# Gated attention levels dealt out head by head between quarters of projection units, with two modulation columns moved one stage later

## The chip, the cores and the metric

The kernel runs on one core of one Trainium2 chip. The metric is the device time of one execution in microseconds; less is better. The core has a matrix engine (TensorE, PE in the rows, its weight loads PEld), a vector engine (VectorE, DVE), a scalar engine (ScalarE, ACT), GpSimd (POOL), and SyncE (SP), whose queue issues almost all transfers from memory.

## The reference, cut to what matters

Two decoder layers over 512 positions of width 1024, in float32. Layer 0 mixes tokens with gated linear attention, layer 1 with latent attention; each is followed by a SwiGLU block, and each sub-layer is normalised and modulated by columns computed from a conditioning vector `c`. Only layer 0's mixer is touched by the change:

```python
mod = silu(c) @ ada_w[i] + ada_b[i]                # 6 x 1024 modulation values per layer
sh1, sc1, g1, sh2, sc2, g2 = split(mod, 6)
h = rmsnorm(x, norm_mix) * (1 + sc1) + sh1
q, k, v, r, glr = split(h @ w_in)                  # 4 heads, DK 128, DV 256
log_a = log_sigmoid(glr @ w_gate + b_gate) / 16    # a decay per position, head and channel
# per head: attn[i, j] = sum_d q[i,d] k[j,d] exp(b[i,d] - b[j,d]) for j <= i, b = cumsum(log_a)
o = rmsnorm(attn @ v, g_out) * silu(r)
x = x + g1 * (o @ w_out)
h = rmsnorm(x, norm_ffn) * (1 + sc2) + sh2          # the next sub-layer needs sc2, sh2
```

## The kernel before, in words

Activations lie transposed, 128 features by 512 positions per tile. Every product is made to float32 accuracy from three passes in a faster type (`mm3`, L178 to L180): each operand is split into a high and a low part, and high x high, high x low and low x high are summed in PSUM. A weight unit (`wunit`, L156) is 128x1024 floats: one load on SP's queue, one cast on ScalarE (L164, `wh`), one subtraction on VectorE (L172, `wl`). Raw, `wh` and `wl` have three buffers each. A unit feeds 24 matmuls of 512 columns.

The gated attention avoids a recurrence by seven **levels** (`LEVELS`, block sizes 1 to 64). At each level and for each of the 4 heads, `level` (L647) multiplies small blocks of k and q on TensorE (16 matmuls of 32x16 for the first five levels, 8 and 4 larger ones for the last two) into a PSUM bank `lv`; VectorE copies the result out (L670, L644), and `decay` (L672) scales half of the rows of q and k on VectorE (L680, L681), which the same head's next level reads. Before the levels `head_setup` (L616) makes each head's diagonal blocks (L626) and `qf`, the decayed copy of q (L632).

The matmuls of this stretch stand in an order written by hand (`manual_schedule` for PE); VectorE, ScalarE and SP have no hand-written order here and are ordered by a scheduler. The hand-written order puts a **fill** after each level: one projection unit of 24 matmuls, so that VectorE can finish all four heads while TensorE works. The fills are the last unit of v's first half, two units of r (`r_tile`, L762), and the four units of v's second half (`v_units`, L723, a generator that yields after each unit).

After the levels come the larger off-diagonal scores (`scores_a`, `scores_b`, L692 to L706), their splits into high and low (`att_split`, `ah` and `al`), the products with v (`pv_head`, tile `pv`), six more units of r with the heads' norms between them (`o_stats`, tile `no_st`, 16 matmuls of one column), and then the output projection (`boundary`, L315): five full units, each followed by a residual update (L290), a square on ScalarE and a sum on VectorE (L268), then the last three units in two halves of 256 positions, with the norm of the first half (`nm_st`) between.

Modulation columns are made on VectorE: `ada` (L136) loads a 128x1024 tile (`adaw`, two buffers), takes its dot product with the conditioning vector (L132) and adds the bias (L141). They wait in one list (`pend_ada`), and `more_ada(n)` takes the next n from it: two in each `r_tile` from the third on, two after each of the first four residuals of the output projection (`also`, L858), three per unit in the SwiGLU block. Columns 9 to 24 of that list are the scale and shift that the SwiGLU block's `modulated` needs.

```python
fill = [lambda: next(v0), lambda: r_tile(0), lambda: r_tile(1), lambda: next(v1), ...]
for li, s in enumerate(LEVELS):
    for hd in range(H):
        level(hd, li, s)
        decay(hd, s)
    fill[li]()
```

Of the kernel before, what the change touches and what calls it, by code (L numbers as in the profile page):

```python
# [21 lines left out]
KD = D // P  # L22
NT = S // P
# [60 lines left out]
def trunk(ctx: ExitStack, tc: tile.TileContext, t: dict, out: bass.AP):  # L84
# [11 lines left out]
    def R(name, dt=F32, cols=S):  # L96
        return ring.tile([P, cols], dt, tag="ring", name=name, bufs=NRING)
# [58 lines left out]
    def wunit(src, n=1024, home=None, split_=True):  # L156
        raw = wp.tile([P, 1024], F32, tag="raw", name="raw")
        nc.sync.dma_start(out=raw[:, :n], in_=src)
        if home is None:
            wh = wp.tile([P, 1024], F32R, tag="wh", name="wh")  # L160
            wl = wp.tile([P, 1024], F32R, tag="wl", name="wl")
        else:
            wh, wl = home
        nc.scalar.copy(out=wh[:, :n], in_=raw[:, :n])  # L164
        w = (wh, wl, raw)
        if split_:
            wunit_lo(w, n)
        return w[:2] if split_ else w
# [13 lines left out]
    def sl(pair, *idx):  # L182
        return pair[0][idx], pair[1][idx]
# [432 lines left out]
    def head_setup(hd):  # L616
        d = heads[hd]
        qs, kr = qk[("q", hd)], qk[("k", hd)]
        if not dqs:
            dqs.append(R("dq"))  # L620
        dq = dqs[0][:, hd * NT * QB:(hd + 1) * NT * QB]
        ps = abank("lv0")
        for i in range(NT):
            for b in range(0, P, QB):
                c = slice(i * P + b, i * P + b + QB)
                nc.tensor.matmul(ps[b:b + QB, i * QB:(i + 1) * QB], lhsT=kr[:, c], rhs=qs[:, c],  # L626
                                 start=i == 0, stop=i == NT - 1, tile_position=(0, b))
        nc.vector.tensor_tensor(out=dq.rearrange("p (a b) -> p a b", b=QB),
                                in0=ps[:, :NT * QB].rearrange("p (a b) -> p a b", b=QB),
                                in1=kc[:, None, K_IDQ:K_IDQ + QB].to_broadcast([P, NT, QB]), op=ALU.mult)  # L630
        qf = R("qf")
        nc.vector.tensor_tensor(out=qf, in0=qs, in1=d["e1"], op=ALU.mult)  # L632
        d.update(kr=kr, qf=qf, dq=dq)
# [89 lines left out]
    def v_units(g):  # L723

        pv = [bank(f"v{i}") for i in range(NT)]
        for u in range(4):
            w = vw.pop((g, u)) if (g, u) in vw else v_load(g, u)
            for kk in range(2):
                k = 2 * u + kk
                for i in range(NT):  # L730
                    mm3(pv[i], sl(h[k], slice(None), slice(i * P, (i + 1) * P)),
                        sl(w, slice(None), slice(kk * S, (kk + 1) * S)), k == 0, k == KD - 1)
            if u == 3:
                for i in range(NT):
                    vt[(g, i)] = split(pv[i], "v")
            yield
# [23 lines left out]
    sr = {}  # L760

    def r_tile(n, cuts=()):  # L762
        w = wunit(t["gla_r"][n])
        if n > 1:
            with tc.issue_after(last["w"]):
                more_ada(2)
        ps = bank("r")
        for k in range(KD):
            mm3(ps, sl(w, slice(None), slice(k * P, (k + 1) * P)), h[k], k == 0, k == KD - 1)
            for k_, f in cuts:  # L770
                if k_ == k:
                    f()
        sr[n] = R("sr")
        nc.scalar.activation(out=sr[n], in_=ps, func=AF.Silu)

    def o_spread(hd):
        o, y = pvs[hd]
# [38 lines left out]
    more_ada(4)  # L816
    with tc.manual_schedule(engines={mybir.EngineType.PE}):
        v0, v1 = v_units(0), v_units(1)
        next(v0)
        ps = abank("qk")  # L820
        proj(ps, w3, h)
        take("k", 3, ps)
        next(v0)
        next(v0)
        for hd in range(H):
            head_setup(hd)
        fill = [lambda: next(v0), lambda: r_tile(0), lambda: r_tile(1), lambda: next(v1), lambda: next(v1),
                lambda: next(v1), lambda: next(v1)]
        for li, s in enumerate(LEVELS):
            for hd in range(H):  # L830
                level(hd, li, s)
                decay(hd, s)
            fill[li]()
        scores_a(0)
        scores_a(1)
        r_tile(2)
        scores_b(0)
        scores_b(1)
        pv_head(0)
        scores_a(2)  # L840
        r_tile(3, [(3, lambda: o_stats(0))])
        scores_b(2)
        pv_head(1)
        scores_a(3)
        r_tile(4, [(1, lambda: o_spread(0)), (3, lambda: o_stats(1))])
        o_out(0)
        scores_b(3)
        pv_head(2)
        r_tile(5, [(1, lambda: o_spread(1)), (3, lambda: o_stats(2))])
        o_out(1)  # L850
        pv_head(3)
        r_tile(6, [(1, lambda: o_spread(2)), (3, lambda: o_stats(3))])
        o_out(2)
        r_tile(7, [(1, lambda: o_spread(3))])
        o_out(3)
    oh = [oh[i] for i in range(KD)]

    def also(n):  # L858
        if n < 4:
            more_ada(2)  # L860


# [431 lines left out]
```

## Time and profile before

| | |
|---|---|
| median of 3 runs | 1183.88 us (1180.38, 1183.88, 1184.00) |
| the profiled execution | 1180.7 us, of which the span from first to last instruction is 1178.9 us |
| TensorE busy | 1154.1 us, 98% of the span, 7070 matmul records |
| VectorE busy | 724.1 us, 61% |
| ScalarE busy | 417.3 us, 35% |
| granted TensorE clock, mean | 0.996 of full speed |
| memory traffic | 130 GB/s over the span |

A small float32 matmul leaves two records, so the 16 matmuls of one head's level show as x32. A matmul's shown duration is longer than its share of the engine, since matmuls overlap; what a matmul costs is the step from its start to the next one's start. A wait is the idle time in front of an instruction, with what ended it behind an arrow; "issue" means that nothing the profile shows ended it. The stretch that the change touches is 87 to 140 us (levels), and then 140 to 248 us (scores, r units, output projection).

### The profile page before, as it was taken

The page shows a single profiled execution, that of the slowest core. Times are in us where ns is not written, and L with a number is a line of the kernel's source. Part 1 is how long each engine was busy: PE and PEld are TensorE (multiplying, and loading weights), DVE is VectorE, ACT ScalarE, POOL GpSimd, SP SyncE. Part 2 cuts the span into 40 slices and gives each one's busy share as a digit, 9 for nine tenths or more (in the row PEclk, how much of TensorE's full clock was granted, in tenths as well). Part 3 has the DMA queues.
Part 4 walks back from the last instruction along what each step waited for, and adds up shares of the span by engine and source line. Part 5 has one row for each costly group of instructions (what it writes and reads, how often), then busy time and mean ns, then how long its engine had stood idle before and what let it go on. Part 6 is the DMA issues. An engine that isn't in the chain of part 4 may idle for free.

```text
span 1178.9 us, 17489 instructions
## 1 busy us (share of the span) xinstructions
PE 1154.1 (98%) x7070; PEld 974.6 (83%) x7070; DVE 724.1 (61%) x1428; ACT 417.3 (35%) x666; POOL 18.1 (2%) x40
## 2 busy tenths in 40 slices
PE   8999999999999999999999899999999999999996
PEld 5877878898888888888899788889888888888886
DVE  6987898875763567556566878757333332333345
ACT  3372445342322222232344556534232222223231
POOL 0000000000000000000000022000000000000000
PEclk9999999999999999999999999999999999999998
DMA  9762264714663567356421224141323333233222
GB/s 355 239 194 57 79 226 127 231 55 146 226 242 101 174 236 244 117 202 231 148 86 51 78 62 107 54 126 31 95 90 97 100 91 100 95 105 93 90 71 72
DMA packets 47379, 156.91 MB, mean 133 GB/s; under 512 B 5602, under 2 KB 8034, under 8 KB 47299
## 3 DMA queue, kind: packets, MB, share of 16 engines
q1 hardware_dynamic: 45474, 153.48, 40.2%
q0 software_dynamic: 1536, 2.10, 0.8%
q8 instruction: 55, 0.90, 0.3%
q10 hardware_dynamic: 288, 0.23, 0.1%
q14 instruction: 26, 0.21, 0.0%
HBM read 151.59 MB, written 2.10 MB: 130 GB/s over the span
## 4 chain that ended last, share of the span: by engine, by line
PE 87%; DVE 7%; DMA 3%; ACT 1%; issue 1%; DVEq 0%; ACTq 0%
PE f L178 12%; PE f L180 12%; PE f L179 12%; PE op L178 9%; PE op L179 8%; PE op L180 8%; PE fg L179 2%; DMA adaw<-in_ada 2%; PE fg L178 2%; PE fg L180 2%; DVE wl L172 1%; DVE junk L132 1%; PE r L178 1%; PE v L178 1%; PE ko L179 1%; PE r L179 1%
## 5 line engine op out<-in xcount | busy, mean ns | idle before, releaser
L164 ACT CAST wh<-raw 128x1024 fp32r<-128x1024 f32 (+2 forms) x173 | 177.5, 1026 | 554.3 <-PE f L179 180.2
L172 DVE TENSOR_TENSOR wl<-raw,wh 128x1024 fp32r<-128x1024 f32 (+2 forms) x181 | 215.4, 1191 | 107.6 <-ACT wh L164 102.1
L178 PE MATMUL f<-hh,wh 128*128 128x512 f32 x640 | 249.0, 389 | 0.0
L179 PE MATMUL f<-hl,wh 128*128 128x512 f32 x640 | 249.0, 389 | 0.0
L180 PE MATMUL f<-hh,wl 128*128 128x512 f32 x640 | 249.0, 389 | 0.0
L178 PE MATMUL op<-acth,wh 128*128 128x512 f32 (+1 forms) x394 | 144.7, 367 | 0.0
L179 PE MATMUL op<-actl,wh 128*128 128x512 f32 (+1 forms) x394 | 144.3, 366 | 0.0
L180 PE MATMUL op<-acth,wl 128*128 128x512 f32 (+1 forms) x394 | 144.3, 366 | 0.0
L180 PEld LDWEIGHTS f<-hh,wl 128*128 128x128 f32 x640 | 120.1, 188 | 25.0
L179 PEld LDWEIGHTS f<-hl,wh 128*128 128x128 f32 x640 | 120.1, 188 | 24.9
L178 PEld LDWEIGHTS f<-hh,wh 128*128 128x128 f32 x640 | 120.1, 188 | 24.8
L290 DVE SCALAR_TENSOR_TENSOR x<-op,mod,x 128x512 f32<-128x512 f32 (+1 forms) x76 | 50.6, 665 | 124.2 <-PE op L180 123.9
L132 DVE SCALAR_TENSOR_TENSOR junk<-adaw,cact 128x1024 bf16<-128x1024 f32 x94 | 114.7, 1220 | 13.8 <-DMA adaw<-in_ada 13.7
L901 DVE TENSOR_TENSOR sg<-sg,f 128x512 f32<-128x512 f32 x40 | 27.5, 688 | 123.5 <-PE f L180 123.5
L178 PEld LDWEIGHTS op<-acth,wh 128*128 128x128 f32 x394 | 74.3, 189 | 12.2
L179 PEld LDWEIGHTS op<-actl,wh 128*128 128x128 f32 x394 | 74.3, 189 | 12.2
L180 PEld LDWEIGHTS op<-acth,wl 128*128 128x128 f32 x394 | 74.3, 189 | 12.1
L268 DVE TENSOR_TENSOR acc<-acc,sq 128x512 f32<-128x512 f32 (+1 forms) x45 | 25.1, 558 | 14.7 <-ACT sq L267 14.6
L280 ACT ACTIVATE hh<-u,mod 128x256 fp32r<-128x256 f32 (+1 forms) x49 | 23.5, 509 | 29.2 <-DVE u L277 29.2
L267 ACT ACTIVATE sq<-x 128x256 f32<-128x256 f32 (+1 forms) x38 | 19.2, 505 | 38.3 <-DVE x L290 38.2
L903 DVE TENSOR_TENSOR actl<-sg,acth 128x512 fp32r<-128x512 f32 (+1 forms) x48 | 30.8, 642 | 0.8 <-ACT acth L902 0.5
L902 ACT CAST acth<-sg 128x512 fp32r<-128x512 f32 (+1 forms) x48 | 28.1, 585 | 6.7 <-DVE sg L901 6.5
(324 smaller groups left out, 1890.8 us busy)
## 6 DMA issues: line engine op xcount, KB each, us to landing
adaw<-in_ada SPq DMA_DIRECT2D x96, 512.0 KB, 4.4
raw<-in_ffn_in SPq DMA_DIRECT2D x80, 512.0 KB, 3.7
raw<-in_ffn_o SPq DMA_DIRECT2D x32, 448.0 KB, 3.3
raw<-in_ffn_o SPq DMA_DIRECT2D x16, 512.0 KB, 3.6
raw<-in_gla_ko SPq DMA_DIRECT2D x8, 512.0 KB, 5.6
raw<-in_gla_v SPq DMA_DIRECT2D x8, 512.0 KB, 4.3
raw<-in_gla_r SPq DMA_DIRECT2D x8, 512.0 KB, 3.9
raw<-in_gla_wo SPq DMA_DIRECT2D x8, 512.0 KB, 3.7
```

What stands on the lines that cost most here:

```text
L132: nc.vector.scalar_tensor_tensor(out=junk, in0=w, scalar=1.0, in1=cact, op0=ALU.mult, op1=ALU.mult, accum_out=acc)
L164: nc.scalar.copy(out=wh[:, :n], in_=raw[:, :n])
L172: ins = nc.vector.tensor_tensor(out=wl[:, :n], in0=raw[:, :n], in1=wh[:, :n].bitcast(F32), op=ALU.subtract)
L178: nc.tensor.matmul(ps, lhsT=ah, rhs=bh, start=start, stop=False)
L179: nc.tensor.matmul(ps, lhsT=ah, rhs=bl, start=False, stop=False)
L180: nc.tensor.matmul(ps, lhsT=al, rhs=bh, start=False, stop=stop)
L268: nc.vector.tensor_tensor(out=self.acc[:, c], in0=self.acc[:, c], in1=sq[:, c], op=ALU.add)
L280: nc.scalar.activation(out=hi[:, c], in_=u[:, c], func=AF.Identity, bias=sh)
L290: ins = nc.vector.scalar_tensor_tensor(out=x[k][:, c], in0=ps[:, c], scalar=mod[l][2 + 3 * j][:, k:k + 1], in1=x[k][:, c], op0=ALU.mult, o ...
L901: ins = nc.vector.tensor_tensor(out=sg[:, c], in0=sg[:, c], in1=pu[:, c], op=ALU.mult)
L902: nc.scalar.copy(out=hi[:, c], in_=sg[:, c])
L903: nc.vector.tensor_tensor(out=lo[:, c], in0=sg[:, c], in1=hi[:, c].bitcast(F32), op=ALU.subtract)
```

## The change

`v_units` and `r_tile` become generators of quarters (six matmuls each). `steps(gen, n)` takes n quarters. In the level loop a quarter of the fill stands behind each head instead of a whole unit behind each level, and two quarters of v's third unit stand among the four head set-ups. `r_tile(2)` loses its two modulation columns, and the output projection takes two more, behind its fifth residual.

```diff
@@ v_units
                         sl(w, slice(None), slice(kk * S, (kk + 1) * S)), k == 0, k == KD - 1)
+                    if i % 2 and (kk, i) != (1, NT - 1):
+                        yield
             if u == 3:
@@
     def r_tile(n, cuts=()):
+        for _ in r_quarters(n, cuts):
+            pass
+
+    def r_quarters(n, cuts=()):
         w = wunit(t["gla_r"][n])
-        if n > 1:
+        if n > 2:
             with tc.issue_after(last["w"]):
                 more_ada(2)
...
+            if k % 2 and k < KD - 1:
+                yield
         sr[n] = R("sr")
         nc.scalar.activation(out=sr[n], in_=ps, func=AF.Silu)
+        yield
@@
-        next(v0)
+        def steps(gen, n):
+            for _ in zip(range(n), gen):
+                pass
+
+        steps(v0, 4)
         ps = abank("qk")
         proj(ps, w3, h)
         take("k", 3, ps)
-        next(v0)
-        next(v0)
+        steps(v0, 6)
         for hd in range(H):
+            steps(v0, 1 if hd < 2 else 0)
             head_setup(hd)
-        fill = [lambda: next(v0), lambda: r_tile(0), lambda: r_tile(1), lambda: next(v1), lambda: next(v1),
-                lambda: next(v1), lambda: next(v1)]
+        fill = [v0, r_quarters(0), r_quarters(1), v1, v1, v1, v1]
         for li, s in enumerate(LEVELS):
             for hd in range(H):
                 level(hd, li, s)
                 decay(hd, s)
-            fill[li]()
+                steps(fill[li], 1)
@@
     def also(n):
-        if n < 4:
+        if n < 5:
             more_ada(2)
```

On TensorE, at the head set-ups and the first level (`v` are the projection's 512-column matmuls, `lv` the small ones, - before and + after):

```order
 L180 MATMUL v_856<-wh,hl 128x512
-L626 MATMUL lv_957<-q,k 32x32 x16
 L626 MATMUL lv_977<-q,k 32x32 x16
 L626 MATMUL lv_997<-q,k 32x32 x16
 L626 MATMUL lv_1017<-q,k 32x32 x16
-L664 MATMUL lv<-qf,k 32x16 x64
+L664 MATMUL lv<-qf,k 32x16 x16
 L178 MATMUL v_853<-wh,hh 128x512
...
 L180 MATMUL v_854<-wh,hl 128x512
+L664 MATMUL lv<-qf,k 32x16 x16
 L178 MATMUL v_855<-wh,hh 128x512
```

One run of 128 small matmuls (four set-ups and the first level) becomes five runs, of 16 (moved up by six 512-column matmuls), 64, 16, 16 and 16. Each of the other six levels, one run before, becomes four. In all 7 runs become 29.

On VectorE, between the scores of the first two heads and the first product with v, before:

```order
L303 TENSOR_TENSOR al_1814<-od_a_1808,ah_1813 128x2x128
L132 SCALAR_TENSOR_TENSOR junk_1833,adac_1834<-adaw_1831,cact_79 128x1024
L172 TENSOR_TENSOR wl_1923<-raw_1920,wh_1922 128x1024
L141 TENSOR_TENSOR mod0_2_97<-adac_1834,cols_76 128x1
L132 SCALAR_TENSOR_TENSOR junk_1928,adac_1929<-adaw_1926,cact_79 128x1024
L172 TENSOR_TENSOR wl_2058<-raw_2055,wh_2057 128x1024
L141 TENSOR_TENSOR mod0_2_97<-adac_1929,cols_76 128x1
L132 SCALAR_TENSOR_TENSOR junk_1934,adac_1935<-adaw_1932,cact_79 128x1024
L303 TENSOR_TENSOR al_1803<-od_b_1864,ah_1802 128x2x256
L303 TENSOR_TENSOR al_1814<-od_b_1869,ah_1813 128x2x256
```

and now:

```order
L303 TENSOR_TENSOR al_1814<-od_a_1808,ah_1813 128x2x128
L132 SCALAR_TENSOR_TENSOR junk_1916,adac_1917<-adaw_1914,cact_79 128x1024
L172 TENSOR_TENSOR wl_2046<-raw_2043,wh_2045 128x1024
L141 TENSOR_TENSOR mod0_2_97<-adac_1917,cols_76 128x1
L132 SCALAR_TENSOR_TENSOR junk_1922,adac_1923<-adaw_1920,cact_79 128x1024
L172 TENSOR_TENSOR wl_2191<-raw_2188,wh_2190 128x1024
L303 TENSOR_TENSOR al_1803<-od_b_1852,ah_1802 128x2x256
L303 TENSOR_TENSOR al_1814<-od_b_1857,ah_1813 128x2x256
```

One dot product fewer stands ahead of `al`; the other that is gone stood in front of the last level's copies. The splits of the diagonal scores (`al<-dg`) now stand between the heads of the last level instead of behind them.

On VectorE, in the output projection behind the fifth unit's residual (`x4_84`; `x5_85` to `x7_87` are the halves that follow), before:

```order
L290 SCALAR_TENSOR_TENSOR x4_84<-op_2745,mod0_2_97,x4_84 128x512
L172 TENSOR_TENSOR wl_2789<-raw_2786,wh_2788 128x1024
L268 TENSOR_TENSOR acc_2516<-acc_2516,sq_2771 128x512
L290 SCALAR_TENSOR_TENSOR x5_85<-op_2811,mod0_2_97,x5_85 128x256
L268 TENSOR_TENSOR acc_2516<-acc_2516,sq_2837 128x256
L290 SCALAR_TENSOR_TENSOR x6_86<-op_2840,mod0_2_97,x6_86 128x256
L268 TENSOR_TENSOR acc_2516<-acc_2516,sq_2866 128x256
L290 SCALAR_TENSOR_TENSOR x7_87<-op_2869,mod0_2_97,x7_87 128x256
```

and now:

```order
L290 SCALAR_TENSOR_TENSOR x4_84<-op_2732,mod0_2_97,x4_84 128x512
L132 SCALAR_TENSOR_TENSOR junk_2763,adac_2764<-adaw_2761,cact_79 128x1024
L268 TENSOR_TENSOR acc_2503<-acc_2503,sq_2758 128x512
L141 TENSOR_TENSOR mod0_4_99<-adac_2764,cols_76 128x1
L172 TENSOR_TENSOR wl_2789<-raw_2786,wh_2788 128x1024
L149 SCALAR_TENSOR_TENSOR gs0_1_108<-mod0_4_99,cols_76 128x1
L132 SCALAR_TENSOR_TENSOR junk_2770,adac_2771<-adaw_2768,cact_79 128x1024
L290 SCALAR_TENSOR_TENSOR x5_85<-op_2811,mod0_2_97,x5_85 128x256
L141 TENSOR_TENSOR mod0_3_98<-adac_2771,cols_76 128x1
L290 SCALAR_TENSOR_TENSOR x6_86<-op_2840,mod0_2_97,x6_86 128x256
L268 TENSOR_TENSOR acc_2503<-acc_2503,sq_2837 128x256
```

Two dot products stand ahead of the first half's residual, one of them ahead of the last weight unit's `wl`. On SP's queue the second one's load stands behind the SwiGLU block's first `in_ffn_in` load.

## Rows read from the trace of the kernel before

**Rows 1.** The page's first part: busy time, share of the span, instructions.
```profile
PE 1154.1 (98%) x7070; PEld 974.6 (83%) x7070; DVE 724.1 (61%) x1428; ACT 417.3 (35%) x666; POOL 18.1 (2%) x40
```

**Rows 2.** Busy time by stretch: us, each engine, granted clock, DMA share, GB/s.
```profile
87.30:140.20 52.90, 50.98 (x1033) 41.85 (x1033) 41.35 (x112) 19.42 (x35) 0.00 (x0) 1.00 0.26 77
```

**Rows 3.** TensorE's waits, 87 to 215 us: us in total, times, longest.
```profile
PE pv L179 <- DVE al L303: 1.6, 1, 1.6
PE lv L664 <- issue: 1.0, 1, 1.0
PE lv L664 <- DVE qf L632: 0.9, 3, 0.4
PE no_st L230 <- DVE acc L268: 0.6, 2, 0.4
```

**Rows 4.** TensorE's timeline, a projection unit, then a level: start, duration, instruction.
```profile
70.98 0.39 PE L178 MATMUL qk<-hh,wh 128*128 128x512 f32 x1
...
76.19 0.39 PE L180 MATMUL qk<-hh,wl 128*128 128x512 f32 x1
...
97.83 0.39 PE L180 MATMUL v<-wh,hl 128*128 128x512 f32 x1
98.15 1.34 PE L664 MATMUL lv<-qf,k 128*32 128x16 f32 x128
99.42 0.50 PE L178 MATMUL r<-hh,wh 128*128 128x512 f32 x1
99.75 0.39 PE L179 MATMUL r<-hl,wh 128*128 128x512 f32 x1
...
105.08 1.34 PE L664 MATMUL lv<-qf,k 128*32 128x16 f32 x128
```

**Rows 5.** TensorE's timeline around the head set-ups and the first level.
```profile
87.07 0.39 PE L180 MATMUL v<-wh,hl 128*128 128x512 f32 x1
...
93.52 0.39 PE L179 MATMUL v<-wl,hh 128*128 128x512 f32 x1
```

**Rows 6.** TensorE's timeline, 16 small matmuls inside a unit of r.
```profile
192.90 0.40 PE L180 MATMUL r<-hh,wl 128*128 128x512 f32 x1
193.23 0.43 PE L230 MATMUL no_st<-ones,acc 128*32 128x1 f32 x32
...
194.64 0.40 PE L179 MATMUL r<-hl,wh 128*128 128x512 f32 x1
```

**Rows 7.** VectorE's timeline ahead of the first product with v.
```profile
148.96 1.23 DVE L132 SCALAR_TENSOR_TENSOR junk<-adaw,cact 128x1024 bf16<-128x1024 f32 x1
...
150.12 1.28 DVE L303 TENSOR_TENSOR al<-od_b,ah 128x512 fp32r<-128x512 f32 x2
```

**Rows 8.** VectorE's timeline in the output projection.
```profile
232.69 1.23 DVE L132 SCALAR_TENSOR_TENSOR junk<-adaw,cact 128x1024 bf16<-128x1024 f32 x1 [0.89 <-DMA adaw<-in_ada]
...
234.51 0.75 DVE L290 SCALAR_TENSOR_TENSOR x<-op,mod,x 128x512 f32<-128x512 f32 x1
235.17 1.22 DVE L172 TENSOR_TENSOR wl<-raw,wh 128x1024 fp32r<-128x1024 f32 x1
...
240.48 0.43 DVE L268 TENSOR_TENSOR acc<-acc,sq 128x256 f32<-128x256 f32 x1 [0.48 <-ACT sq L267]
```

**Rows 9.** TensorE's timeline in the output projection: the last unit's first half, the norm.
```profile
236.44 0.38 PE L180 MATMUL op<-ohh,wl 128*128 128x256 f32 x1 [0.18 <-DVE wl L172]
...
242.14 0.31 PE L230 MATMUL nm_st<-ones,acc 128*32 128x1 f32 x16
```

**Rows 10.** The tile adaw, 205 to 245 us: its loads.
```profile
DMA to landing us min/median/max: 3.6/4.6/5.9
```

**Rows 11.** Busy time by stretch near the end, columns as in rows 2.
```profile
1170.00:1172.00 2.00, 1.22 (x4) 0.93 (x4) 0.97 (x6) 0.00 (x0) 0.00 (x0) 0.50 0.08 26
```

**Rows 12.** TensorE's timeline near the end: the same two matmuls (four records) twice.
```profile
1163.77 0.60 PE L246 MATMUL nf_bc<-kc,rs_f 128*128 128x128 f32 x4
...
1170.67 1.22 PE L246 MATMUL nf_bc<-kc,rs_f 128*128 128x128 f32 x4 [2.45 <-DVE rs_f L215]
```

## The prediction

> **What bounds the kernel now.** I read the busy shares first [rows 1]: TensorE is busy 98% of the span and VectorE 61%, so a change must shorten TensorE's own sequence or one of its few waits. The busy times by stretch come next [rows 2]: in the levels, 87.3 to 140.2 us, TensorE has 50.98 of 52.90 us, VectorE 41.35. TensorE's waits from 87 to 215 us [rows 3] are all that a new order can win there: 1.0 + 0.9 us at the head set-ups and the first level, 1.6 us at the first product with v, 0.6 us at the heads' norms. From the second level to the last there is none: VectorE has caught up before the next level starts. So the question is what the new order costs TensorE itself, and for that its timeline must be read step by step [rows 4 to 6].
>
> **A run of small matmuls between large ones.** A 512-column matmul takes 0.2265 us of TensorE: 23 steps lie between 70.98 and 76.19 [rows 4]. One level's run starts at 98.15, the next at 105.08, with 24 large matmuls between: 6.93 - 24 x 0.2265 = 1.49 us for a run of 64 small ones. The trace also has a run of 16 small ones inside a unit [rows 6]: from 192.90 to 194.64 lie five large steps and the run, 1.74 - 5 x 0.2265 = 0.61 us. These 16 have one column where a level's have 16, but they come in the same 32-column blocks. So 16 cost 0.61 and 64 cost 1.49: the 48 more cost 0.88, 0.29 per 16, and 0.32 us is paid once per run, however short. The level's own edges say where: 0.32 us instead of 0.23 from the last large matmul to the first small one, and 0.33 instead of 0.23 from the first large one to the second [rows 4]. These two edges alone make 0.09 + 0.10 = 0.19 us; that is my lower end for the price of a run. I take 0.32, because the 16-run is the very thing that the change makes.
>
> The Trainium skill (TensorE: Matmul & The Clock Gate, "The mechanism") says that TensorE pulls a weight load ahead of matmuls in flight when it goes to other row groups or to the background weight buffer. By that a run's edge would cost nothing, the levels' term below would be zero and the whole sum -1.8 us. The trace disagrees at these edges, with 0.10 us extra on the first large step.
>
> **The change, part by part.**
>
> *Levels two to seven.* Six runs become 24; the small and large matmuls are the same ones. 18 more runs x 0.32 = **+5.7 us** (lower end 18 x 0.19 = 3.4). Nothing hides it, as TensorE is the engine that is waited for. VectorE is busy 41.35 us over the seven levels [rows 2], 5.9 us a level at most, and a level now lasts about 7.9 us, so I add no wait between levels.
>
> *Head set-ups and first level.* From 87.07 to 93.52 lie five large steps and everything else: 6.45 - 1.13 = 5.32 us [rows 5], the waits on `qf` and "issue" included. The same 128 small matmuls now stand in runs of 16, 64, 16, 16 and 16: 0.61 + 1.49 + 3 x 0.61 = 3.93 us. `qf` no longer arrives late, since the order on VectorE gives the first head's `qf` while six large matmuls run. **-1.4 us.** If the "issue" wait comes back, -0.4.
>
> *First product with v.* TensorE waits 1.6 us for `al` [rows 3], which starts at 150.12 because a dot product stands before it from 148.96 [rows 7]; a dot thus takes about 1.15 us from its start to the next start. One dot fewer stands there now, and the two splits `al<-dg` have gone ahead of the last head. Against that, ScalarE's new order puts a weight cast between the casts `vh` of the last v unit, so `vl`, and with it all that follows on VectorE, starts later. I take half of the dot, **-0.5 us**, between 0 and -1.6.
>
> *Heads' norms.* The 0.6 us on `acc` [rows 3] are a sum on VectorE that comes late. With two dots fewer in front of it I take **-0.4 us** (0 to -0.6).
>
> *Output projection.* The two columns come back as two dots behind the fifth residual, which began at 234.51 [rows 8]. Before, the last unit's `wl` followed at 235.17, and TensorE already waited for it: 0.18 us, until 236.44 [rows 9]. Now the first dot (1.15 us) and the sum `acc` (about 0.6 us, estimated from the half-width one of 0.43 [rows 8]) stand ahead of that `wl`, and TensorE stands for them in full: 1.75, **+1.8 us**, between +0.5 (if that `wl` moves up with a VectorE that has less to do) and +2.9 (a dot more). The second dot stays covered. Its load is issued when the dot that ran from 232.69 has freed its buffer, at 233.84, and lands 3.6 to 5.9 us later [rows 10], median 4.6: at 238.4, just after the late `wl`. The dot ends near 239.6. The three first halves took VectorE from 236.9 (235.17, a `wl` of 1.15 and the sum of 0.6) to 240.9 (240.48 + 0.43 [rows 8]), 4.0 us, so they end by 243.6. `nm_st` needs them at 242.14 [rows 9] + 1.8 = 243.9. If this cover is gone, the rest of the dot counts too.
>
> The last modulation columns are still done before `modulated` uses them, and from there on the list of columns, the units and the queues are as before: zero.
>
> **The sum.** 5.7 - 1.4 - 0.5 - 0.4 + 1.8 = +5.2 us on the profiled execution, 1180.7 to 1185.9 us. The median of the runs shown is 1183.88, 3.2 us above that execution, with one of three runs at its level; I take the median as the base: **1189.1 us**, +0.44%. A difference under 0.3%, 3.55 us, can't be told from none with this kernel; the forecast lies on the slower side of that.
>
> **The rivals.**
>
> *Not slower, because a run's edge is nearly free.* If what rows 6 show is due to their one-column matmuls, and a level's short run is cheaper, the 22 extra runs cost little. At no cost per run the sum is 5.2 - 22 x 0.32 = -1.8, 1182.1 us; below about 0.24 us a run the change can't be told from none, below 0.08 it costs nothing. For it: the 16-run has another form. Against it: the level's own two edges show 0.19 us, and the 0.32 comes from two rows together. 15%, mostly for part of the effect. The skill's rule on weight loads pulled ahead would lead here.
>
> *Same, because VectorE, two dots lighter, is early everywhere.* All of the 1.6 and 0.6 us behind the levels go, and the output projection's `wl` is only 0.5 us later: 5.2 - 1.1 - 0.2 - 1.3 = +2.6 us, 1186.5 us. For it: VectorE's order has the splits earlier. Against it: the cast that now delays `vl`, and that the fifth residual came late in the row because of a dot's load, which two dots fewer before do not move. 20%.
>
> *Clearly slower, because the second dot isn't covered.* Its load stands on SP's queue behind a SwiGLU weight load, which itself waits for a raw buffer. If it lands at the slow end, 1.3 us later, or waits for that buffer, the three first halves end 1.0 to 2.3 us after `nm_st` could run, some 1.7: 5.2 + 1.7 = +6.9, 1190.8 us. 18%.
>
> *Much slower, because the clock falls.* More edges mean more short gaps. At the kernel's end, after 2.45 us without work, the granted clock is 0.50 [rows 11], the 1.2 GHz level, and the same two matmuls take 1.22 us instead of 0.60 [rows 12]. One unit of 24 large matmuls at that level costs 5.4 us more: 1194.5 us at least. Against it: the clock is 1.00 throughout the levels [rows 2], even across the set-ups' 1.9 us of waits. 2%. The Trainium skill (same page, "A second HAM failure mode: psum-queue depth-cycling") tells of a kernel whose short gaps between matmul groups made the clock go back and forth; no row here shows it within the levels.
>
> That the order isn't what the diff says is excluded: in the built order TensorE has 29 runs.
>
> **How the numbers follow.** The forecast has 40%, the four rivals 15, 20, 18 and 2%, the rest is unknown. Slower by over 0.3%: nine tenths of the forecast's 40, the 18, the 2 and the smallest part of the second case, near 0.6. Same: most of the 15 and the 20, and a tenth of the forecast, 0.32. Faster by over 0.3% needs free edges and all waits gone at once, 0.08. With the lower price of a run (22 x 0.13 = 2.9 less) and the second rival's gains the sum is -0.3; with the second dot uncovered it is +6.9. On the median that is 1183.6 to 1190.8; as the runs themselves differ by 3.6 us, I put the range at 1182.5 to 1192.
>
> **What would show it.** In the changed profile: 29 runs of small matmuls, each x32 run taking about 0.61 us between large matmuls; a level's period of about 7.9 instead of 6.93 us; no `qf` or "issue" wait at the set-ups; the wait `pv <- al` near 1.1 us; the wait `op <- wl` in the output projection near 2 us instead of 0.18; `nm_st` without a wait on `acc`. The prediction is wrong if the period stays under 7.4 us, if TensorE waits for VectorE between levels, or if the output projection shows no wait on `wl`.

## The result, and the profile after

Eight runs of the changed kernel beside eight of the one before gave a median of 1186.54 us (1184.43 to 1188.18) against 1183.94 us (1180.38 to 1185.09): a ratio of 1.0028, 95% interval 1.0019 to 1.0038. A second timing, 12 runs beside 17, gave 1186.97 against 1183.62 us, ratio 1.0029 (1.0015 to 1.0043). So the change makes the kernel slower, by 0.28% and 0.29%, which is 3.3 and 3.4 us. The ratio is not the quotient of the two medians: these lie 2.6 and 3.4 us apart, 0.22% and 0.28%. The slowdown is just under the 0.3% that the forecast called the least that can be told from no change, though both intervals exclude none. The forecast was 1189.1 us, +0.44%; the direction is right, the size too large.

The profiled execution of the changed kernel took 1186.36 us, with a span of 1184.6 us; TensorE is busy 98% of it, as before [rows 1]:

```profile
PE 1162.1 (98%) x7070; PEld 974.7 (82%) x7070; DVE 725.6 (61%) x1428; ACT 417.2 (35%) x666; POOL 18.0 (2%) x40
```

Busy time by stretch, from the end of the last matmul before the first head's set-up to the first scores, answers to [rows 2] (columns: stretch, its length, then PE, PEld, DVE, ACT, POOL, granted clock, DMA share, GB/s):

```profile
86.05:144.96 58.91, 58.91 (x1040) 42.30 (x1039) 42.70 (x111) 19.03 (x34) 0.00 (x0) 1.00 0.23 73
```

TensorE stands still nowhere in it, and yet it lasts longer: 58.91 us, less the six large matmuls that moved in (6 x 0.2265 = 1.36), is 57.6 us against 52.9. The time went into TensorE's own work, not into a wait. The engine's waits from 80 to 260 us answer to [rows 3]; `qf` and "issue" are gone, `al` and `acc` shorter, and one is longer, `wl` in the output projection:

```profile
PE pv L179 <- DVE al L303: 0.9, 1, 0.9
PE op L180 <- DVE wl L172: 0.8, 1, 0.8
PE pv L178 <- ACT ah L302: 0.2, 1, 0.2
PE no_st L230 <- DVE acc L268: 0.2, 1, 0.2
```

One head's run in TensorE's timeline, between a quarter of v and one of r (start, duration, instruction; to be read beside [rows 4]):

```profile
96.57 0.40 PE L180 MATMUL v<-wh,hl 128*128 128x512 f32 x1
96.90 0.45 PE L664 MATMUL lv<-qf,k 128*32 128x16 f32 x32
97.28 0.50 PE L178 MATMUL r<-hh,wh 128*128 128x512 f32 x1
97.61 0.40 PE L179 MATMUL r<-hl,wh 128*128 128x512 f32 x1
...
98.54 0.40 PE L180 MATMUL r<-hh,wl 128*128 128x512 f32 x1
98.87 0.45 PE L664 MATMUL lv<-qf,k 128*32 128x16 f32 x32
```

From 96.57 to 98.54 are six large steps and one run: 1.97 - 6 x 0.2265 = 0.61 us a run, and 4 x 1.97 = 7.88 us a level.

**Three stretches.** To compare many kernels I cut TensorE's timeline at four instructions: the first matmul of the last k unit (`qk`), the first scores (`od_a`), the first matmul of the output projection (`op`) and the first norm in it (`nm_st`). **A** is from `qk` to `od_a`, **B** from there to `op`, **C** from there to `nm_st`. For the kernel before, `qk` stands at 70.98 [rows 4] and `nm_st` at 242.14 [rows 9]; the two others are:

```profile
140.29 0.27 PE L692 MATMUL od_a<-qf,k 128*128 128x128 f32 x1
...
202.85 0.39 PE L178 MATMUL op<-ohh,wh 128*128 128x512 f32 x1
```

And for the changed kernel:

```profile
71.08 0.39 PE L178 MATMUL qk<-hh,wh 128*128 128x512 f32 x1
...
144.96 0.38 PE L692 MATMUL od_a<-qf,k 128*128 128x128 f32 x2
...
206.22 0.39 PE L178 MATMUL op<-ohh,wh 128*128 128x512 f32 x1
...
246.17 0.31 PE L230 MATMUL nm_st<-ones,acc 128*32 128x1 f32 x16
```

A went from 69.31 to 73.88 us (+4.57), B from 62.56 to 61.26 (-1.30), C from 39.29 to 39.95 (+0.66): +3.9 us together. The two spans differ by 5.7 us. Most of the rest is in layer 1, which the change does not touch: in the changed kernel's profile the granted clock fell there for a short time. Busy time by stretch and TensorE's timeline of the product `qr`:

```profile
670.30:673.40 3.10, 3.10 (x7) 2.46 (x8) 2.33 (x4) 0.60 (x2) 0.00 (x0) 0.50 0.43 127
```

```profile
668.95 0.51 PE L178 MATMUL qr<-cqh,wh 128*128 128x512 f32 x1 [1.43 <-ACT cqh L199]
670.29 0.79 PE L179 MATMUL qr<-cql,wh 128*128 128x512 f32 x1 [0.83 <-DVE cql L200]
670.88 0.63 PE L180 MATMUL qr<-cqh,wl 128*128 128x512 f32 x1
...
673.75 0.40 PE L178 MATMUL qr<-cqh,wh 128*128 128x512 f32 x1
```

After waits of 1.43 and 0.83 us the clock is 0.50 (the 1.2 GHz level) for about 3 us, and matmuls that take 0.23 us elsewhere take some 0.43 us each; the product takes 1.6 us longer than in the profile of before, which has the same two waits and a clock of 1.00. The experiments ask whether that belongs to the change.

### The profile page after: what moved, and what is told of

Same layout as the page of the kernel before. It is cut to its first block, busy times and chain, and to the rows that moved or that the text cites. A ratio compares the mean times of both kernels' runs of the same rounds, so it can differ in the third digit from the quotient of the medians.

```text
span 1184.6 us, 17488 instructions
## 1 busy us (share of the span) xinstructions
PE 1162.1 (98%) x7070; PEld 974.7 (82%) x7070; DVE 725.6 (61%) x1428; ACT 417.2 (35%) x666; POOL 18.0 (2%) x40
## 4 chain that ended last, share of the span: by engine, by line
PE 89%; DVE 7%; DMA 2%; ACT 1%; issue 1%; POOL 0%; SPq 0%; DVEq 0%; ACTq 0%
PE f L179 12%; PE f L180 12%; PE f L178 12%; PE op L178 8%; PE op L179 8%; PE op L180 8%; PE fg L179 2%; PE fg L178 2%; PE fg L180 2%; PE v L178 2%; DVE wl L172 2%; PE r L178 1%; PE v L180 1%; PE v L179 1%; DVE junk L132 1%; PE r L180 1%
## 5 line engine op out<-in xcount | busy, mean ns | idle before, releaser
L917 DVE TENSOR_TENSOR actl<-sg,acth 128x512 fp32r<-128x512 f32 (+1 forms) x48 | 30.8, 642 | 0.7 <-ACT acth L916 0.5
```

What stands on the lines that cost most here:

```text
L917: nc.vector.tensor_tensor(out=lo[:, c], in0=sg[:, c], in1=hi[:, c].bitcast(F32), op=ALU.subtract)
```

## The experiments

All times in us; A, B and C come from each kernel's own profile, in the way shown above. Each ratio is to runs of the kernel before that were timed beside that kernel (their medians lie between 1182.6 and 1183.9), so it can't be worked out from the medians in the table.

| kernel | A | B | C | median (runs) | ratio to before, interval |
|---|---|---|---|---|---|
| before | 69.31 | 62.56 | 39.29 | 1183.94 (8) | |
| before again | 69.09 | 63.94 | 38.87 | 1182.74 (10) | 0.9998 (0.9983 to 1.0012) |
| changed | 73.88 | 61.26 | 39.95 | 1186.54 (8) | 1.0028 (1.0019 to 1.0038) |
| changed again | 73.85 | 61.31 | 39.82 | 1186.97 (12) | 1.0029 (1.0015 to 1.0043) |
| interleaving only | 73.85 | 61.69 | 38.86 | 1185.06 (10) | 1.0012 (0.9998 to 1.0026) |
| columns only | 69.31 | 60.91 | 40.04 | 1181.46 (10) | 0.9983 (0.9965 to 1.0001) |
| first level only | 68.15 | 62.53 | 38.87 | 1180.96 (10) | 0.9983 (0.9963 to 1.0002) |
| halves | 69.27 | 60.87 | 39.77 | 1180.82 (10) | 0.9980 (0.9965 to 0.9995) |
| eighths | 79.04 | 61.27 | 40.19 | 1190.47 (1) | one run |
| two runs | 69.01 | 60.87 | 40.74 | 1184.16 (12) | 1.0020 (1.0005 to 1.0036) |
| full width | 80.31 | 61.27 | 40.06 | 1195.78 (1) | one run |
| few level runs | 67.15 | 62.68 | 38.86 | 1180.53 (12) | 0.9979 (0.9969 to 0.9988) |
| the same, columns as before | 67.23 | 62.21 | 38.87 | 1180.70 (12) | 0.9984 (0.9972 to 0.9997) |

**Interleaving only**: the changed kernel, with the two columns put back.

```diff
-        if n > 2:
+        if n > 1:
...
-        if n < 5:
+        if n < 4:
```

> The change's interleaving alone; the two modulation columns stay where they were. Three stretches of TensorE's timeline are compared with before and the changed kernel: A, from the first matmul of k's last projection unit (tile qk) to the first score matmul (od_a): 69.31 us before, 73.88 changed; B, from there to the output projection's first matmul (op): 62.56 and 61.26; C, from there to the first norm matmul (nm_st): 39.29 and 39.95. Theory (each run of small matmuls costs TensorE about 0.32 us; the columns move B and C): A about 73.9, B about 62.5, C about 39.3, some +4.6 us in all. Rival 1 (the new order itself, with the splits of the diagonal scores between the heads, shortened B): B about 61.3. Rival 2 (VectorE, with two more dots again, becomes late within the quartered levels): A above 74.5 with waits of lv on qf or on k.

A is 73.85, as with the columns moved, and no wait shows in it: the whole rise of A is the interleaving's, and rival 2 falls. C is 38.86. B is neither of the two numbers, but 61.69; there the first product with v waits 0.5 us for `al` instead of 1.6 [rows 3], so part of B's gain comes from the order.

**Columns only**: the kernel before with `n > 2` and `n < 5`.

> The kernel before with the two columns moved, no interleaving. Theory (columns move B and C, runs move A): A about 69.3, B about 61.3 (the first product with v waits 0.9 instead of 1.6 us, the heads' norm 0.2 instead of 0.6), C about 40.0 (op waits for wl 0.8 instead of 0.2), some -0.6 us in all. Rival (B was shortened by the order, not by the columns): B about 62.5, C 40.0, +0.7 us.

A is untouched, B falls by 1.65, C rises. So either half of the change shortens B, and the two do not add up: 61.26 with both. In C the wait of `op` on `wl` is 0.9 us.

**First level only**: quarters up to the first level, then whole units, columns as before.

```diff
-                steps(fill[li], 1)
+                if li == 0:
+                    steps(fill[li], 1)
+            if li:
+                steps(fill[li], 4)
```

> Quarters only among the head set-ups and in the first level; from the second level on whole units stand behind whole levels, and the columns stay as before. Theory (a run costs 0.32 us wherever it stands, and the set-ups' waits were worth 1.4 net): A = 73.88 - 18 x 0.32 = 68.1 us, 1.2 less than before; B about 62.5, C 39.3; some 1.2 us less in all. Rival (the later levels' quarters cost because of something else than their number of runs, such as a later start of VectorE's work): A does not come back below 69.3 us.

A is 68.15, within 0.1 us of the theory. The 18 runs that are gone were worth 73.85 - 68.15 = 5.70 us, 0.317 each, and the interleaving at the set-ups by itself gains 1.2 us.

**Halves**: two heads, then 12 large matmuls.

```diff
-                steps(fill[li], 1)
+                if hd % 2:
+                    steps(fill[li], 2)
```

> The changed kernel with halves: two heads, then twelve large matmuls. Levels two to seven have 12 runs of small matmuls instead of 24, the first level two instead of four. Theory (a fixed price per run): A = 73.88 - 14 x 0.32 = 69.4 us; a half's period is 12 x 0.2265 + 0.32 + 2 x 0.29 = 3.62 us. Rival (the price goes by the number of small matmuls next to large ones, or lies in waits between a head's decay and its next level): A stays near 73.9, or falls at once to about 68.

A is 69.27: 14 runs fewer, 4.61 us, 0.33 each. With that the change as a whole is no loss any more: the three stretches are 169.9 us together, against 171.2 and 171.9 in the two profiles of before, and the ratio is 0.9980.

**Eighths**: three large matmuls between runs of 8 (the generators yield after each k or i, and `level` takes a step after the second of its four position tiles).

> The changed kernel with every head's run of 16 small matmuls cut into two runs of 8, three large matmuls between, in levels two to five (the levels with 16 small matmuls a head): 16 runs more. Theory (0.32 us for a run, whatever its length): A = 73.9 + 16 x 0.32 = 79.0 us, a run of 8 takes 0.32 + 0.145 = 0.47 us of TensorE beyond the large steps. Rival 1 (only the two edges that are seen, 0.10 + 0.10 us, belong to the run, the rest to the small matmuls): A = 73.9 + 16 x 0.2 = 77.1 us. Rival 2 (the price goes by the small matmuls): A stays at 73.9.

A is 79.04: 16 runs more, 5.16 us, 0.32 each. In TensorE's timeline three large steps and a run of 8 now take 1.15 us, 0.47 more than the large steps alone:

```profile
98.28 0.32 PE L666 MATMUL lv<-qf,k 128*32 128x16 f32 x16
98.52 0.51 PE L178 MATMUL r<-hh,wh 128*128 128x512 f32 x1
...
99.43 0.32 PE L666 MATMUL lv<-qf,k 128*32 128x16 f32 x16
```

From 11 runs to 45 the price of a run is the same 0.32 us, whether it holds 64, 32, 16 or 8 small matmuls. Both rivals fall. The rows also show where the part lies that the two edges of the prediction don't account for: from a run's first small matmul to the next large one it takes 0.24 us for 8 small matmuls, 0.38 for 16 and 1.27 for 64 [rows 4], each time some 0.1 us more than 0.29 us per 16 would give.

**Before again.**

> The kernel before, unchanged, run as if it were a change. Theory: A 69.3, B 62.6, as in its first profile; C is 38.9 instead of 39.3 if the load that came late ahead of the fifth residual there (0.89 us of waiting) was an accident of that execution, and 39.3 if it belongs to the kernel. Where the granted clock drops (0 to 70 us, and at the product qr of layer 1) is a matter of the execution: the ratio's interval holds 1.000, while single runs differ by several us. Rival: the drop at qr, seen in the changed kernel's profile alone so far, comes from the change, and the runs of before do not reach its mean clock of 0.993.

The interval holds 1.000. C is 38.87, so the 0.4 us more of the first profile were an accident of that execution. B, though, is 63.94, with 1.9 us of waiting at one head's norm. VectorE's timeline shows where from: the load of a modulation tile lands late, and the head's sum stands behind its dot product in VectorE's order.

```profile
155.98 1.23 DVE L132 SCALAR_TENSOR_TENSOR junk<-adaw,cact 128x1024 bf16<-128x1024 f32 x1 [1.95 <-DMA adaw<-in_ada]
...
158.60 0.68 DVE L268 TENSOR_TENSOR acc<-acc,sq 128x512 f32<-128x512 f32 x1
```

And `qr` shows the lower clock in this profile of before too (0.75 from 665 to 670 us and 0.91 from 670 to 675). So the drop does not come from the change.

**Two runs**: a first attempt at a better version. Level one of all heads directly behind the last three set-ups, and the two columns spread over the last unit of r and the first residual.

```diff
-                more_ada(2)
+                more_ada(3 if n == 7 else 2)
...
-            steps(v0, 1 if hd < 2 else 0)
+            steps(v0, 1 if hd == 1 else 0)
...
-                steps(fill[li], 1)
+            steps(fill[li], 4 if li else 5)
...
-        if n < 5:
-            more_ada(2)
+        if n < 4:
+            more_ada(2 if n else 3)
```

> A version from what the first experiments showed: the first head's set-up, six large matmuls, then the other three set-ups and all four heads of level one as one run of 112; whole units behind whole levels from there on. r_tile(2) makes no modulation column, r_tile(7) makes three instead of two and the first residual of the output projection three instead of two, none stands behind the fifth residual. Theory: A = 68.16 - 3 x 0.32 = 67.2 us (level one's runs merged); B about 60.9 as with the columns moved; C about 38.9 with no wait of op on wl; in all 4.2 us less than before's profile, ratio about 0.9965. Rival 1 (qf of the last heads comes late again): A about 68.2 or more, with waits of lv on qf. Rival 2 (the extra dot products in r_tile(7) and at the first residual delay wl or the heads' norms): B or C about 1 us longer.

Both rivals came true. TensorE's waits from 80 to 245 us:

```profile
PE op L180 <- DVE wl L172: 1.6, 1, 1.6
PE lv L664 <- DVE qf L632: 0.9, 3, 0.4
...
PE lv L664 <- issue: 0.3, 1, 0.3
```

Six large matmuls ahead of the set-ups of three heads do not cover those heads' `qf`. And VectorE's third dot product behind the first residual had to wait 1.01 us for its load; the dots fell behind by one, two of them stood ahead of the fifth residual instead of one, and TensorE waited for `wl` behind it.

**Full width**: in levels one to five each run of 16 small matmuls in 32-column tiles becomes four that use all 128 columns; the scores of these levels are not computed.

```diff
-            for b in range(0, P, QB):
-                c = slice(i * P + b, i * P + b + QB)
...
+            nc.tensor.matmul(ps[:, i * nq:(i + 1) * nq], lhsT=kr[:, i * P:(i + 1) * P],
...
```

> The changed kernel with each run of 16 small matmuls (tiles of 32 columns of the array) of levels one to five replaced by 4 matmuls that use all 128 columns, with 16 moving columns each; the scores of those levels are therefore not computed rightly. It asks where the edges of a run come from. Theory (the change of tile width makes the entry edge): the step from the last large matmul to the run's first is 0.23 us instead of 0.33, and from the run's first large matmul to the next 0.31 instead of 0.33, as at od_b and no_bc, which are 128 wide. Rival (any small float32 matmul after large ones makes it): 0.33 and 0.33 as now.

TensorE's timeline around one such run:

```profile
98.17 0.39 PE L180 MATMUL v<-wh,hl 128*128 128x512 f32 x1
98.40 0.96 PE L662 MATMUL lv<-qf,k 128*128 128x16 f32 x8
99.21 0.48 PE L178 MATMUL v<-wh,hh 128*128 128x512 f32 x1
99.53 0.39 PE L179 MATMUL v<-wl,hh 128*128 128x512 f32 x1
```

The entry step is 0.23 us, the exit step 0.32, as the theory has it: the 0.10 us at the entry are gone with the 32-column tiles, those at the exit are there at either width. (The number of matmuls in the run changes too, from 16 to four; which of the two removes the entry edge was not tested apart.) The run itself is longer, 0.81 us for the four, so nothing is gained by it.

**Few level runs.** From what the two-runs version showed: all set-ups as one run, 12 large matmuls behind them as cover for `qf`, level one as one run, whole units from there on, and the two columns in the last two units of r.

```diff
         for hd in range(H):
-            steps(v0, 1 if hd < 2 else 0)
             head_setup(hd)
+        steps(v0, 2)
...
-                steps(fill[li], 1)
+            steps(fill[li], 4)
...
-                more_ada(2)
+                more_ada(3 if n > 5 else 2)
...
-        if n < 5:
+        if n < 4:
```

> The four head set-ups as one run, two quarters of v's third unit behind them (they cover qf, which takes VectorE about 3.4 us for four heads), level one of all heads as one run, and from there on whole units behind whole levels: 8 runs in all. r_tile(2) makes no modulation column, r_tile(6) and r_tile(7) make three instead of two, the output projection is as before. Theory: set-ups and level one take 1.49 + 1.49 us besides the large steps instead of 5.32, A = 69.3 - 2.3 = 67.0; B about 60.9 as with the columns moved; C 38.9 with no wait of op on wl; 4.4 us less than before's first profile, ratio 0.996. Rival 1 (qf of the later heads comes late even behind twelve large matmuls): A 67.5 to 68.5, with waits of lv on qf. Rival 2 (as in the version with two runs, a third dot product behind one unit makes a load wait, and the delay is carried on to the fifth residual): C 40 or more, or B above 61.5.

Faster than both kernels, with a ratio to before of 0.9979 (0.9969 to 0.9988). TensorE's timeline has the set-ups and level one as two runs of 1.28 and 1.42 us from their start to the next large matmul, with no wait:

```profile
84.45 1.35 PE L626 MATMUL lv<-q,k 128*32 128x32 f32 x128
85.73 0.50 PE L178 MATMUL v<-wh,hh 128*128 128x512 f32 x1
...
88.67 1.49 PE L664 MATMUL lv<-qf,k 128*32 128x16 f32 x128
90.09 0.50 PE L178 MATMUL v<-wh,hh 128*128 128x512 f32 x1
```

A (67.15) and C are as expected. B is not, and rival 2 comes true there: the third head's norm waits. TensorE's row and VectorE's, in this version:

```profile
180.15 0.43 PE L230 MATMUL no_st<-ones,acc 128*32 128x1 f32 x32 [1.94 <-DVE acc L268]
```

```profile
179.32 0.68 DVE L268 TENSOR_TENSOR acc<-acc,sq 128x512 f32<-128x512 f32 x1
```

The same sum in the two-runs version:

```profile
179.21 0.68 DVE L268 TENSOR_TENSOR acc<-acc,sq 128x512 f32<-128x512 f32 x1
```

Counted from `qk`, which stands at 70.76 and 70.58, that is 108.6 us in both, although TensorE is through with A 1.9 us sooner here; A and B together are 129.83 and 129.88 us. In both, two dot products and a split stand directly ahead of the sum. So what A gained over the two-runs version B gave back. That VectorE's order alone sets the time there is not shown, as VectorE also waited on the way to this sum: 0.78 us for the load of a dot product at 166.86 us in this version, 0.57 us for TensorE (`od_b`) at 172.41 us in the two-runs version.

**The same, columns as before**: only the first two edits of that diff, with `n > 1` and `n < 4`.

> The same, with all modulation columns as in the kernel before. Theory: A 67.0; C 38.9; B as in before, which two of its profiles give as 62.6 and 63.9 (the wait of the heads' norms on a sum that stands behind dot products whose load comes late): 3 to 4 us less than before's profiles of the same kind, ratio about 0.998. Rival (the moved columns gain nothing that lasts, and in the median this version is as fast as the one with moved columns): the two medians within 0.5 us.

A and C are as expected, B is 62.21, and the medians of the two versions are 0.2 us apart: in the time, the rival holds. What the two have in common, few runs and cover for `qf`, is faster than before; on top of it, moving the columns adds nothing that the medians show. By their ratios, 0.9979 to 0.9984, five versions can't be told apart: columns only, first level only, halves and these two. The three stretches together put these two first: 168.3 us with the columns as before and 168.7 with them moved, then 169.6 (first level only), 169.9 (halves) and 170.3 (columns only).

**Changed again.**

> The changed kernel, unchanged, a second time. The three stretches say that the change costs 3 to 4 us (171.2 and 171.9 us in before's two profiles, 175.1 in the changed one), the first timing said 2.6 us with an interval of 2.2 to 4.5. Theory (the stretches are right, and the first medians were taken at a different mix of mean clocks): A 73.9, B 61.3, C 39.9 to 40.2, the ratio of the medians between 1.0025 and 1.0040, and runs with the same mean clock 4 us apart. The drop of the clock at qr is there in some executions of either kernel, so it may be missing in this profile. Rival (something outside these stretches gives 1 us back in the timed runs): the ratio is below 1.0022 again, and runs with the same mean clock are less than 3 us apart.

A, B and C come back within 0.13 us, and the ratio as well. Much of the spread of the runs goes with the clock: the median of before's runs goes from 1187.3 us at a mean clock of 0.989 (4 runs) to 1179.9 at 0.996 (12), though runs with the same mean clock still differ by up to some 3 us. Over all timings, with the mean granted clock of each run where it is on record: at 0.993, before 1182.9 us (20 runs) and changed 1187.6 (8), 4.7 apart; at 0.994, 1183.7 (24) and 1186.6 (3), 2.9; at 0.995, 1182.1 (21) and 1185.8 (7), 3.8; at 0.996, 1179.9 (12) and 1185.0 (1), 5.1. All of them, 104 and 20 runs, have medians of 1183.1 and 1186.7, 3.5 apart. The theory said 4 us at the same clock; these differences lie around it, with one, of three changed runs, just under 3. With a ratio of 1.0029 the rival falls. It also fits the stretches: 175.1 and 175.0 us in the changed kernel's two profiles, 171.2 and 171.9 in before's, 3.1 to 3.9 us. The clock of the runs of before spreads further down, to 0.989, the changed kernel's to 0.993; why is open, as no profile of such a run exists.

## Why the prediction was right in direction and too high in size

**The price of a run: right.** 0.32 us, from a run of 64 and a run of 16 with one column [rows 4, 6], held for every count and length tried (0.317, 0.33 and 0.32). The lower end, 0.19 from the visible edges alone, would have put A of the eighths 2 us lower than it came out; the 0.1 us that it left out lies in the run itself. The rival of the free edge falls. TensorE's weight loads in the changed kernel, of the last large matmul of a quarter (which runs from 96.57) and of the run behind it (from 96.90), show it:

```profile
96.34 0.19 PEld L180 LDWEIGHTS v<-wh,hl 128*128 128x128 f32 x1
96.90 0.35 PEld L664 LDWEIGHTS lv<-qf,k 128*32 128x32 f32 x32 [0.37 <-issue]
```

The large one's load starts 0.23 us ahead of its matmul; the run's first load starts only with the run's first matmul. The Trainium skill (TensorE: Matmul & The Clock Gate, "The mechanism") says that weight loads are pulled ahead of matmuls in flight. The trace agrees between large matmuls, with these 0.23 us, and disagrees at a run's entry.

**Levels two to seven: right**, +5.7 forecast, 5.70 measured between interleaving only and first level only.

**Set-ups and first level: right**, -1.4 forecast. The changed kernel's five runs take about 3.96 us by its timeline, against 3.93 forecast; in A it is -1.2 (68.15 against 69.31; -0.9 against the 69.09 of before's second profile).

**First product with v and heads' norms: right in sign.** -0.5 and -0.4 were forecast; the waits went from 1.6 to 0.9 and from 0.6 to 0.2, and B by -1.3 in all. What I did not see is that the base of the second is not a fixed number: in another execution of the same kernel that wait was 2.1 us. The order alone brings the first wait to 0.5, the columns alone too, and both together only to 0.9. The reason that I gave for taking half of a dot is in the changed kernel's rows, on VectorE and on ScalarE: VectorE waits for `vh`, whose cast stands behind a weight cast.

```profile
146.72 1.45 DVE L200 TENSOR_TENSOR vl<-v,vh 128x512 fp32r<-128x512 f32 x2 [0.36 <-ACT vh L199]
```

```profile
145.16 1.05 ACT L164 CAST wh<-raw 128x1024 fp32r<-128x1024 f32 x1 [1.62 <-PE v L180]
146.11 0.58 ACT L199 CAST vh<-v 128x512 fp32r<-128x512 f32 x1
```

This wait of 0.36 us stands in the second profile of the changed kernel and in the eighths too, and in these three `al<-od_b` starts 9.1 us after `od_a`. In interleaving only, columns only and halves `vl` has no such wait, and `al` starts 8.7 us after. That no version moves this cast alone leaves it untested by itself.

**Output projection: the step that failed.** It said that TensorE already waited for the last unit's `wl` [rows 9] and would therefore stand for the dot product and the sum in full, +1.8 us. C rose by 0.66 against the first profile, by 1.1 against the second. VectorE's timeline in the changed kernel:

```profile
236.34 0.74 DVE L290 SCALAR_TENSOR_TENSOR x<-op,mod,x 128x512 f32<-128x512 f32 x1
237.37 1.23 DVE L132 SCALAR_TENSOR_TENSOR junk<-adaw,cact 128x1024 bf16<-128x1024 f32 x1 [0.29 <-DMA adaw<-in_ada]
...
238.52 0.69 DVE L268 TENSOR_TENSOR acc<-acc,sq 128x512 f32<-128x512 f32 x1
...
239.20 1.22 DVE L172 TENSOR_TENSOR wl<-raw,wh 128x1024 fp32r<-128x1024 f32 x1
...
241.16 1.23 DVE L132 SCALAR_TENSOR_TENSOR junk<-adaw,cact 128x1024 bf16<-128x1024 f32 x1 [0.68 <-DMA adaw<-in_ada]
```

The fifth residual begins 236.34 - 206.22 = 30.1 us after `op`; in the row on which I built, 234.51 - 202.85 = 31.7 us [rows 8], behind a dot that had waited 0.89 us for its load. That wait is in the row, and I took it for a part of the kernel. In the second profile of before no dot waits there, `op` stands at 203.90, and the residual and `wl` come 30.69 and 31.35 us after it:

```profile
234.59 0.74 DVE L290 SCALAR_TENSOR_TENSOR x<-op,mod,x 128x512 f32<-128x512 f32 x1
235.25 1.22 DVE L172 TENSOR_TENSOR wl<-raw,wh 128x1024 fp32r<-128x1024 f32 x1
```

There TensorE does not wait for `wl`, and C is 38.87. So TensorE stands only for what puts `wl` later than a certain time after `op`. All thirteen profiles agree on it: in the five where `op` does not wait for `wl`, `wl` begins at most 31.6 us after `op` and C is 38.86 or 38.87; in the eight where it waits, `nm_st` begins 6.97 to 6.99 us after `wl` does. 38.87 - 6.97 = 31.9 us, so a `wl` up to 31.9 us after `op` is free.

In the changed kernel `wl` would have followed the residual after 0.66 us, as in both profiles of before, at 30.8, 1.1 us early. What was put ahead of it is 2.2 us: the dot and the sum that I had priced, 1.8, and 0.4 more as the dot waited for its load. Half of that was hidden: `wl` began at 239.20 - 206.22 = 33.0, 1.1 us too late, and that is what C rose by against the second profile of before. Of these 1.1 us the profile shows 0.81 as a wait, since a matmul's shown duration is longer than its step; in the first profile of before `wl` at 32.3 cost 0.4 us in C, of which 0.18 is shown.

The end of +0.5 that I gave for a `wl` that moves up was the nearer one. The dot and the sum do stand ahead of `wl`, as forecast: every profile with a dot behind the fifth residual has a C of 39.8 to 40.2, every one with the columns elsewhere 38.9, apart from before's first (39.3) and the two-runs version (40.7). The second dot waits for its load (0.68 us) but is covered, and `nm_st` waits for nothing, so the rival that it isn't covered falls. TensorE's wait:

```profile
240.47 0.38 PE L180 MATMUL op<-ohh,wl 128*128 128x256 f32 x1 [0.81 <-DVE wl L172]
```

**The sum and the base.** +5.2 forecast, +3.9 and 3.1 in the stretches of the profiles: against before's first profile C accounts for 1.1 of the difference and B for 0.4, while A rose by 0.3 more than forecast. The rival with VectorE early everywhere named the output projection's earlier `wl`, which is the right place, but its time, 1186.5 us, agrees with the median measured, 1186.54, by luck: its condition, that all of the waits behind the levels go, did not hold (0.9 and 0.2 us of them are left), and its sum of +2.6 us is less than any of the stretches and ratios show.

**The clock in the levels** stayed at 1.00, so that rival falls as well. The drop seen in layer 1 is in profiles of both kernels.

## What to carry to other kernels

When work is dealt out more finely on the engine that bounds the kernel, count the changes of matmul shape first: here each run of 32-column matmuls between 512-column ones cost 0.32 us, however short, so 8 runs with cover where it was missing beat 29. A wait that the profile shows once, with a transfer behind it, may be that execution's own: look at what released it and take a second execution before building a term of the sum on it. Cover pays only where the engine waits: twelve large matmuls moved between the set-ups and the first level took 2 us off their stretch, while 18 more pieces in levels without a wait cost 5.7.

## What was not expected

The price of a run is the same to about 0.01 us over runs of 8 to 64 small matmuls, and of its two visible edges only the one at the entry went away with the 32-column tiles (0.33 us with them, 0.23 with full width; 0.33 and 0.32 at the exit).

The granted clock fell in some executions and not in others at two places. One is `qr`, where it was 0.50 for about 3 us in the changed kernel's profile and cost 1.6 us there. The clock fell at `qr` in seven of the thirteen profiles, among them the second one of before and both of the changed kernel, and the waits ahead of it, 1.4 and 0.8 us, are the same in all thirteen; what decides it there is open. The other place is in the first 20 us, ahead of layer 0's first projection, in the profiles of interleaving only, columns only and full width; in the first of these, most of the later start of `qk` (72.82 instead of 70.98 us) comes from it:

```profile
14.00:20.00 6.00, 5.38 (x18) 2.84 (x14) 1.95 (x9) 1.43 (x3) 0.00 (x0) 0.72 1.03 416
```

Here the executions differ before the clock falls. In these three TensorE had waited 0.5 to 0.9 us for VectorE at `n_st`, in interleaving only so:

```profile
12.48 0.43 PE L499 MATMUL n_st<-ones,sq 128*32 128x1 f32 x32 [0.47 <-DVE sq L482]
```

Eight of the other profiles have no wait there, and the clock stays at 1.00 in them. It also stays in the eighths (0.3 us of waiting) and in the two-runs version (0.9 us), so the wait alone does not settle it.
